# A two-layer hybrid decoder: products with V in pairs, branch weights split two tiles at once, two changes of order

## The chip, the cores and the metric

One core of a Trainium2 chip runs the whole kernel in one launch. The metric is the device time of that launch in microseconds (us); of several runs the median is taken.

## The reference, cut to what matters

Two layers, each on x of 512 tokens by 1024 channels, all in float32:

```
x = x + 1/2 SwiGLU(RMSNorm(x))
u = RMSNorm(x);  one projection u @ w_in feeds four branches and four merge gates
  A  sliding-window attention (8 heads, 2 K/V groups, window 128, sinks)
  B  gated short convolution
  C  three attentions (compressed, selected, windowed), 8 heads, 2 K/V groups, sigmoid gates
  D  retention, 4 heads, chunks of 128, group norm, swish gate
x = x + w_out( sum_b sigmoid(gate_b) * (y_b @ w_branch_b) )
x = x + 1/2 SwiGLU(RMSNorm(x))
```

Softmax rows P are multiplied with V: for each of the two K/V groups, `out[query, 64] += P[query, 128 keys] @ V[128 keys, 64]`, for four heads at once.

## The kernel before, in words

**Precision.** Weight matrices come in as float32 and are split in two by `split` (L206 to L215): ScalarE writes `whi` (L213), VectorE writes the rest, `wlo = raw - whi` (L214). Activations are split alike, so one product is three matmuls. `whi` and `wlo` have two buffers each in the pool `wp`; while `ph["two"]` holds, splits alternate between `wp` and the pool `fp`.

**Order.** The kernel is written through a framework that lists every engine's instructions by their place in the program and a planner's estimate of when each is ready, and then fixes that order. Every engine executes its own list strictly in order. `tc.issue_after(ins)` places an engine's later instructions behind `ins`.

**The mixer of a layer** (function `mixer`) goes in this program order: `swa_prep`, `swa` (branch A), `merge(1)` (branch B), `retention` (D), `merge(0)`, `nsa` (C), `merge(3)`, `merge(2)`, then w_out. What is later in the program fills gaps of what is earlier: the matmuls of a merge (L231 gate projections, L818 branch products) lie between the instructions of the attentions.

**Products with V** (`pv_acc`, L1070 to L1087). For block j of 128 keys, `turn(j)` makes for each group g four transposes of P on TensorE (L1076) into one PSUM tile `tp` (2 buffers), and one ScalarE copy to `PT` (L1078, 3 buffers). Then one matmul per group (L1086), V of 64 columns stationary, PT of 512 columns moving; group 0 writes partitions 0 to 63 of one PSUM tile `pv`, group 1 partitions 64 to 127. `turn(j + 1)` stands in the program ahead of the matmuls of j. Being float32, a matmul is recorded as two instructions. There are 1, 2, 2, 2 blocks for the four query blocks of `swa` and twice 1, 2, 3, 4 for those of `nsa`: 27 pairs in a layer.

**Merges** (`merge`). For each of 8 output tiles d: the gate (projected, or for `(b, c)` in `slots`, that is (2,0), (2,1), (1,1), (0,1), fetched by a GpSimd DMA into `th`, 2 buffers, L791), a split of a 512-wide piece of w_branch, 12 matmuls (L818), and on VectorE the gating and the sum into `merged` (L822, L823). In `merge(2)` the function `out_in` splits each finished `merged[d]` into a pair of halves of tiles `b` (L1253, L1254).

**w_out** (`out_unit`). Pool `mx`, which holds `merged`, is left and `fp` opened. Eight units d, each 24 matmuls over k = 0 to 7 (L1280); k needs the halves of `merged[k]`. The weights of four units are prepared ahead of the first.

**Retention's end.** `nsa` stands in `issue_after(mark["ret"].ins)`. `mark["ret"]` is the last transpose of retention's last chunk (L952), which needs `on` of VectorE (L948, L949), computed from `po` (L921, L923).

Of the kernel before, what the change touches and what calls it, by code (L numbers as in the profile page):

```python
# [12 lines left out]
AF = mybir.ActivationFunctionType  # L13
OP = mybir.AluOpType
AX = mybir.AxisListType

T = 512
D = 1024
NT = T // 128
KT = D // 128  # L20
# [51 lines left out]
def body(tc, ins, out):  # L72
# [620 lines left out]
    def mixer(l, spill, F):  # L693
# [89 lines left out]
        def merge(b, y, perm, done=None):  # L783
            yh, yl = y
            wb = ins["w_branch"][l, b]
            gen = weights_fm(w_in, O_MG + b * D, KT if (b, 1) not in slots else KT // 2)

            def gate(d):
                if (b, d // 4) in slots:
                    z = mp.tile([128, T], F32, name="th", tag="th", bufs=2)  # L790
                    pool.dma_start(z, gated[l][:, slots[b, d // 4] * 4 + d % 4])  # L791
                    return z
                ps = mm_t()
                dot(ps, next(gen), A, ks, True, True)
                z = mp.tile([128, T], F32, name="th", tag="th", bufs=2)
                dve.tensor_tensor(z, ps, R, op=OP.mult)
                act.activation(z, z, AF.Tanh, scale=0.5, bias=vcol("merge_gate_bias", (l * 4 + b) * KT + d))
                return z

            for c in range(2):  # L800
                raw = raw_t().rearrange("p (k n) -> p k n", k=4)
                cs = slice(c * 512, (c + 1) * 512)
                loaded = False
                for d in range(4 * c, 4 * c + 4):
                    z = gate(d)
                    if not loaded:
                        loaded = True
                        if perm:
                            for g in range(2):
                                sp.dma_start(raw[g * 64:(g + 1) * 64], wb[g * 256:(g + 1) * 256, cs].rearrange("(r d) n -> d r n", d=64))  # L810
                        else:
                            sp.dma_start(raw, wb[:, cs].rearrange("(k p) n -> p k n", p=128))
                    s = d - 4 * c
                    whi, wlo = split(raw[:, :, s * 128:(s + 1) * 128], (4, 128))
                    ps = mm_t()
                    for k in range(4):
                        for j, (x, v) in enumerate(((whi, yh), (whi, yl), (wlo, yh))):
                            pe.matmul(ps, x[:, k], v[:, k], start=k == 0 and j == 0, stop=k == 3 and j == 2)  # L818
                    if merge.first:
                        dve.scalar_tensor_tensor(merged[:, d], z, 1.0, ps, op0=OP.add, op1=OP.mult)  # L820
                    else:
                        dve.scalar_tensor_tensor(z, z, 1.0, ps, op0=OP.add, op1=OP.mult)  # L822
                        dve.tensor_tensor(merged[:, d], merged[:, d], z, op=OP.add)  # L823
                    if done:
                        done(d)
            merge.first = False
# [11 lines left out]
        def retention(ps_q, ps_k, ps_v, ps_g):  # L838
# [54 lines left out]
            for i in range(NT):  # L893
                rot, t = qk[i // 2][:, i % 2], sx[i // 2][:, i % 2]
                rf, tf = rot.rearrange("p h d -> p (h d)"), t.rearrange("p h d -> p (h d)")
                ps = tp_t()
                for c in range(4):
                    pe.transpose(ps[:, c * 128:(c + 1) * 128], rf[:, c * 128:(c + 1) * 128], ident)
                qkT = w2()
                act.activation(qkT, ps, AF.Copy)  # L900
                if i:
                    ps = tp_t()
                    for c in range(2):
                        pe.transpose(ps[:, c * 128:(c + 1) * 128], tf[:, c * 128:(c + 1) * 128], ident)
                    qxT = w2()
                    act.activation(qxT[:, :256], ps[:, :256], AF.Copy)

                at = w2()
                for par in range(2):
                    b0 = par * 64  # L910
                    ps = sc_t()
                    for c in range(2):
                        cs = slice(c * 128, (c + 1) * 128)
                        pe.matmul(ps[:, cs], qkT[b0:b0 + 64, 256 + c * 128:256 + (c + 1) * 128], qkT[b0:b0 + 64, cs], start=True, stop=True)
                    dve.tensor_tensor(at.rearrange("p (c q t) -> p c q t", c=2, q=2)[:, :, par], ps[:, :256].rearrange("p (c t) -> p c t", c=2),
                                      dmask.rearrange("p (c q) t -> p c q t", c=2)[:, :, par], op=OP.mult)
                po = pv_t()
                vi = v[i // 2][:, i % 2]
                for h in range(RH):
                    hs = slice(h * 128, (h + 1) * 128)  # L920
                    pe.matmul(po[:, hs], at[:, hs], vi[:, hs], start=True, stop=i == 0)  # L921
                    if i:
                        pe.matmul(po[:, hs], qxT[:, (h // 2) * 128:(h // 2 + 1) * 128], S[:, h], start=False, stop=True)  # L923
                if i < NT - 1:
                    ps = tp_t()
                    for h in range(RH):
                        b0 = (h % 2) * 64
                        pe.matmul(ps[b0:b0 + 64, (h // 2) * 128:(h // 2 + 1) * 128], t[:, 4 + h, :], vi[:, h * 128:(h + 1) * 128], start=True, stop=True)
                    for h in range(RH):
                        rows, c = slice((h % 2) * 64, (h % 2) * 64 + 64), h // 2  # L930
                        src = ps[rows, c * 128:(c + 1) * 128]
                        if i == 0:
                            dve.tensor_copy(S[rows, h], src)
                        else:
                            dve.scalar_tensor_tensor(S[rows, h], S[rows, h], C["decay"][rows, c:c + 1], src, op0=OP.mult, op1=OP.add)
                bs = small([128, RH * 6], name="bs", bufs=2).rearrange("p (h s) -> p h s", h=RH)
                mv = small([128, RH * 2], name="mv", bufs=2).rearrange("p (h s) -> p h s", h=RH)
                for h in range(RH):
                    dve.bn_stats(bs[:, h], po[:, h * 128:(h + 1) * 128])
                for h in range(RH):  # L940
                    dve.bn_aggr(mv[:, h], bs[:, h])
                vv = small([128, RH], name="vv", bufs=2)
                dve.tensor_scalar(vv, mv[:, :, 1], EPS, None, op0=OP.add)
                rs = rsqrt(vv, RH)
                on = w2()
                for h in range(RH):
                    hs = slice(h * 128, (h + 1) * 128)
                    dve.tensor_scalar(on[:, hs], po[:, hs], mv[:, h, 0:1], rs[:, h:h + 1], op0=OP.subtract, op1=OP.mult)  # L948
                dve.tensor_tensor(on, on, g[i // 2][:, i % 2], op=OP.mult)  # L949
                ps = tp_t()  # L950
                for h in range(RH):
                    mark["ret"] = pe.transpose(ps[:, h * 128:(h + 1) * 128], on[:, h * 128:(h + 1) * 128], ident)  # L952
                put_y(ps, (yh, yl), i)
            return (yh, yl), gates

# [114 lines left out]
        def pv_acc(pv, P, nblk, V, first, last):  # L1070
            def turn(j):
                pts = []
                for g in range(2):
# [1 line left out]
                    for r in range(4):  # L1075
                        pe.transpose(ps[:, r * 128:(r + 1) * 128], P[4 * g + r][:, j * 128:(j + 1) * 128], ident)  # L1076
                    pt = aq.tile([128, 512], F32, name="PT", tag="PT", bufs=3)
                    act.activation(pt, ps, AF.Copy)  # L1078
                    pts.append(pt)
                return pts  # L1080

            pts = turn(0)
            for j in range(nblk):
                nxt = turn(j + 1) if j + 1 < nblk else None
                for g in range(2):
                    pv_last[0] = pe.matmul(pv[g * 64:(g + 1) * 64], V(g, j), pts[g], start=first and j == 0, stop=last and j == nblk - 1)  # L1086
                pts = nxt  # L1087

        def swa_prep():
            return q_prep(O_AQ) + kv_prep(proj_tm(O_AK, 256), 1, [G["swa_k"]])  # L1090
# [177 lines left out]
        def out_unit(d):  # L1268
# [3 lines left out]
                return split(raws[d // 2][:, :, d % 2 * 128:(d % 2 + 1) * 128], (KT, 128), d < 4)  # L1272

            def run(w):
                whi, wlo = w
                ps = mm_t()
                for k in range(KT):
                    hi, lo = (t[k // 2][:, k % 2] for t in m)
                    for j, (x, v) in enumerate(((whi, hi), (whi, lo), (wlo, hi))):
                        pe.matmul(ps, x[:, k], v, start=k == 0 and j == 0, stop=k == KT - 1 and j == 2)  # L1280
                dve.scalar_tensor_tensor(XT[d], ps, 0.5, XT[d], op0=OP.mult, op1=OP.add)
                norm_in(d, vcol("ffn2_norm", l * KT + d), True)

            return prep, run

# [95 lines left out]
```

## Time and profile before

| what | value |
|---|---|
| median of 3 runs | 2796.18 us (2795.99 to 2796.74) |
| the profiled execution | 2791.7 us |
| its span, first to last instruction | 2789.9 us |
| granted TensorE clock, mean | 0.994 |
| DMA: moved, mean rate | 291.25 MB, 104 GB/s |

Stages of layer 1 in the span: attention A 555 to 608 us, retention 690 to 757, attention C 855 to 975, `merge(2)` 983 to 1009, w_out from 1014; layer 2 has the same some 1382 us later. A timeline row gives start, duration, engine, line, output<-inputs and a count where neighbours are merged; what stands in brackets is the idle time ahead of it and what ended that.

### The profile page before, as it was taken

The numbers are of one execution on the slowest core, as the hardware profiler recorded it, in microseconds if no ns is written. First come the engines' busy times: TensorE is split into PE (matmuls) and PEld (weight loads), VectorE is DVE, ScalarE is ACT, GpSimd is POOL, SyncE is SP. The second block draws the span as 40 slices with busy tenths as digits, with TensorE's granted clock in tenths as the row PEclk, the third lists the DMA queues.
The fourth block names the chain that finished last, engine by engine and source line by source line (L and its number), as shares of the span: only waits on it lengthen the run. The fifth ranks groups of instructions, "written<-read, shape, count | busy, mean of one in ns | idle before, by whom it ended". The sixth has DMA issues, their size and how long they took to land.

```text
span 2789.9 us, 42565 instructions
## 1 busy us (share of the span) xinstructions
PE 2751.5 (99%) x17303; PEld 2380.6 (85%) x17303; DVE 2087.7 (75%) x3490; ACT 1354.1 (49%) x2152; POOL 63.9 (2%) x70
## 2 busy tenths in 40 slices
PE   7999999999999989999999999999999999999999
PEld 7999999878776579999999998998787766799997
DVE  8887899664757569786897868896557575788874
ACT  7443565453246545443554435555432465554443
POOL 0000000000000010000000000000000000100000
PEclk9999999999999999999999999999999999999999
DMA  5233324414232052333323333334233221532322
GB/s 169 91 108 115 119 98 155 158 59 121 76 121 61 1 185 88 106 108 105 110 87 108 97 99 126 126 127 146 89 91 106 91 61 39 174 106 91 97 86 76
DMA packets 243336, 291.25 MB, mean 104 GB/s; under 512 B 8060, under 2 KB 211652, under 8 KB 241092
## 3 DMA queue, kind: packets, MB, share of 16 engines
q1 hardware_dynamic: 235604, 273.78, 30.3%
q0 software_dynamic: 3136, 12.59, 1.4%
q8 instruction: 135, 2.21, 0.3%
q10 hardware_dynamic: 4400, 2.17, 0.3%
q14 instruction: 61, 0.50, 0.1%
HBM read 269.64 MB, written 18.87 MB: 103 GB/s over the span
## 4 chain that ended last, share of the span: by engine, by line
PE 60%; DVE 2%; ACT 1%; issue 0%; DMA 0%; ACTq 0%; POOL 0%; DVEq 0%; POOLq 0%
PE sc L432 16%; PE mm L562 12%; PE tp L432 8%; PE mm L231 5%; PE pv L432 4%; PE mm L1280 3%; PE mm L818 3%; PE mm L777 3%; PE pv L1086 2%; PE tp L1076 1%; PE pv L777 1%; PE sc L1038 1%; PE sc L1039 1%; DVE wlo L214 0%; DVE Alo L343 0%
## 5 line engine op out<-in xcount | busy, mean ns | idle before, releaser
L213 ACT ACTIVATE whi<-raw 128x1024 fp32r<-128x1024 f32 (+2 forms) x354 | 337.2, 954 | 596.9 <-PE mm L562 122.4
L214 DVE TENSOR_TENSOR wlo<-raw,whi 128x1024 fp32r<-128x1024 f32 (+2 forms) x354 | 384.4, 1091 | 164.3 <-ACT whi L213 157.6
L562 PE MATMUL mm<-h,whi 128*128 128x512 f32 x1408 | 442.8, 395 | 0.0
L213 ACT ACTIVATE whi<-s 128x1024 fp32r<-128x1024 f32 x232 | 246.0, 1060 | 337.7 <-PE sc L432 77.5
L214 DVE TENSOR_TENSOR wlo<-s,whi 128x1024 fp32r<-128x1024 f32 x232 | 282.4, 1219 | 48.0 <-ACT whi L213 47.3
L562 PEld LDWEIGHTS mm<-h,whi 128*128 128x128 f32 x1408 | 259.9, 188 | 59.2 <-DVE h L549 0.2
L432 PE MATMUL sc<-E,whi 128*128 128x256 f32 x1856 | 297.0, 282 | 0.0
L562 PE MATMUL mm<-h,wlo 128*128 128x512 f32 x704 | 277.9, 395 | 0.0
L432 PEld LDWEIGHTS sc<-E,whi 128*128 128x128 f32 x1856 | 254.4, 191 | 0.0
L432 PE MATMUL sc<-E,wlo 128*128 128x256 f32 x928 | 186.5, 282 | 0.1
L566 DVE SCALAR_TENSOR_TENSOR XT<-mm,XT 128x512 f32<-128x512 f32 x128 | 88.0, 687 | 124.5 <-PE mm L562 124.5
L231 PE MATMUL mm<-Ahi,whi 128*128 128x512 f32 x416 | 167.8, 403 | 0.0
L432 PE MATMUL sc<-Ahi,whi 128*128 128x256 f32 x816 | 164.5, 283 | 3.3 <-ACT whi L213 3.3
L231 PE MATMUL mm<-Alo,whi 128*128 128x512 f32 x416 | 166.4, 400 | 0.0
L231 PE MATMUL mm<-Ahi,wlo 128*128 128x512 f32 x416 | 166.2, 400 | 0.0
L432 PE MATMUL sc<-Ahi,wlo 128*128 128x256 f32 x816 | 163.7, 282 | 0.5 <-DVE wlo L214 0.5
L432 PE MATMUL sc<-Alo,whi 128*128 128x256 f32 x816 | 163.9, 282 | 0.0
L562 PEld LDWEIGHTS mm<-h,wlo 128*128 128x128 f32 x704 | 132.0, 187 | 32.1
L213 ACT ACTIVATE whi<-rawd 128x1024 fp32r<-128x1024 f32 (+1 forms) x96 | 94.7, 988 | 131.4 <-PE sc L432 64.3
L432 PE MATMUL tp<-E,whi 128*128 128x256 f32 x928 | 147.8, 281 | 0.3 <-ACT sn L419 0.3
L432 PEld LDWEIGHTS sc<-E,wlo 128*128 128x128 f32 x928 | 143.8, 191 | 0.3 <-DVE wlo L214 0.3
L438 DVE TENSOR_TENSOR s<-raw 128x1024 f32<-128x1024 f32 x116 | 141.2, 1217 | 3.7 <-DMA raw<-in_ffn_w_up_dram 2.9
(318 smaller groups left out, 6113.3 us busy)
## 6 DMA issues: line engine op xcount, KB each, us to landing
raw<-in_w_in_dram SPq DMA_DIRECT2D x66, 1024.0 KB, 6.1
raw<-in_ffn_w_gate_dram SPq DMA_DIRECT2D x44, 1024.0 KB, 5.2
raw<-in_ffn_w_up_dram SPq DMA_DIRECT2D x44, 1024.0 KB, 7.7
rawd<-in_ffn_w_down_dram SPq DMA_DIRECT2D x32, 1024.0 KB, 5.3
rawd<-in_ffn_w_down_dram SPq DMA_DIRECT2D x16, 768.0 KB, 4.4
gs<-O SPq DMA_DIRECT2D x8, 1024.0 KB, 3.9
raw<-in_w_branch_dram SPq DMA_DIRECT2D x8, 1024.0 KB, 8.3
th<-gs POOLq DMA_DIRECT2D x32, 256.0 KB, 3.0
```

The lines of the kernel that those rows point to most:

```text
L213: act.activation(hi, src, AF.Copy)
L214: dve.tensor_tensor(lo, src, fv(hi), op=OP.subtract)
L231: pe.matmul(ps, x, y, start=first and j == 0, stop=last and j == len(passes) - 1)
L432: pe.matmul(ps[:, g * 256:(g + 1) * 256], x[:, g * 4 + c], factor(u, s, c), start=first and n == 0, stop=last and n >= 22, skip_group_chec ...
L438: dve.tensor_tensor(t, a, b, op=OP.add)
L562: pe.matmul(ps, x[:, k, j * 128:(j + 1) * 128], h[:, s, b], start=k == 0 and n == 0, stop=k == nf - 1 and n == 2)
L566: dve.scalar_tensor_tensor(XT[d], ps, 0.5, XT[d], op0=OP.mult, op1=OP.add)
L777: pe.matmul(ps[i][:, :n], a, w, start=kk == 0 and j == 0, stop=kk == KT - 1 and j == 2)
L818: pe.matmul(ps, x[:, k], v[:, k], start=k == 0 and j == 0, stop=k == 3 and j == 2)
L1038: pe.matmul(ps[:, :n], q, kT[0][:, g, s0:s0 + n], start=True, stop=False)
L1086: pv_last[0] = pe.matmul(pv[g * 64:(g + 1) * 64], V(g, j), pts[g], start=first and j == 0, stop=last and j == nblk - 1)
L1280: pe.matmul(ps, x[:, k], v, start=k == 0 and j == 0, stop=k == KT - 1 and j == 2)
```

## The change

Four edits. (1) In `pv_acc` the matmul of group 0 gets a dependency on the ScalarE copy of group 1, so that both matmuls of a block are ready together. (2) In `merge`, for tiles whose gates are fetched, a split takes 256 columns (two tiles) at a time. (3) In w_out, unit 0 stops after k = 5, unit 1 does k = 0 to 5, then unit 0 and unit 1 do k = 6 and 7. (4) `mark["ret"]` becomes the last chunk's last matmul of attention with V (L921) in place of the last transpose.

```diff
+SYNC = mybir.DependencyInfo(mybir.DependencyClass.Sync, mybir.DependencyReason.DATA)
...
-                    whi, wlo = split(raw[:, :, s * 128:(s + 1) * 128], (4, 128))
+                    if (b, c) in slots:
+                        if s % 2 == 0:
+                            two = split(raw[:, :, s * 128:(s + 2) * 128], (4, 256))
+                        whi, wlo = (t[:, :, s % 2 * 128:(s % 2 + 1) * 128] for t in two)
+                    else:
+                        whi, wlo = split(raw[:, :, s * 128:(s + 1) * 128], (4, 128))
...
-                    pe.matmul(po[:, hs], at[:, hs], vi[:, hs], start=True, stop=i == 0)
+                    mark["ret"] = pe.matmul(po[:, hs], at[:, hs], vi[:, hs], start=True, stop=i == 0)
...
-                    mark["ret"] = pe.transpose(ps[:, h * 128:(h + 1) * 128], on[:, h * 128:(h + 1) * 128], ident)
+                    pe.transpose(ps[:, h * 128:(h + 1) * 128], on[:, h * 128:(h + 1) * 128], ident)
...
-                    act.activation(pt, ps, AF.Copy)
+                    last_copy[0] = act.activation(pt, ps, AF.Copy)
                     pts.append(pt)
-                return pts
-
-            pts = turn(0)
+                return pts, last_copy[0]
+
+            last_copy = [None]
+            pts, copied = turn(0)
             for j in range(nblk):
-                nxt = turn(j + 1) if j + 1 < nblk else None
+                nxt = turn(j + 1) if j + 1 < nblk else (None, None)
                 for g in range(2):
                     pv_last[0] = pe.matmul(pv[g * 64:(g + 1) * 64], V(g, j), pts[g], start=first and j == 0, stop=last and j == nblk - 1)
-                pts = nxt
+                    if g == 0:
+                        tc.add_manual_dep(pv_last[0].ins, copied.ins.name, SYNC, reason="pair")
+                pts, copied = nxt
...
             def run(w):
-                whi, wlo = w
+                def mms(ps, w, k0, k1):
+                    whi, wlo = w
+                    for k in range(k0, k1):
+                        hi, lo = (t[k // 2][:, k % 2] for t in m)
+                        for j, (x, v) in enumerate(((whi, hi), (whi, lo), (wlo, hi))):
+                            pe.matmul(ps, x[:, k], v, start=k == 0 and j == 0, stop=k == KT - 1 and j == 2)
+
+                def done(d, ps):
+                    dve.scalar_tensor_tensor(XT[d], ps, 0.5, XT[d], op0=OP.mult, op1=OP.add)
+                    norm_in(d, vcol("ffn2_norm", l * KT + d), True)
+
                 ps = mm_t()
+                if d < 2:
+                    mms(ps, w, 0, KT - 2)
+                    if d == 0:
+                        raws["kept"] = ps, w
+                        return
+                    p0, w0 = raws.pop("kept")
+                    mms(p0, w0, KT - 2, KT)
+                    done(0, p0)
+                    mms(ps, w, KT - 2, KT)
+                else:
+                    mms(ps, w, 0, KT)
+                done(d, ps)
...
```

## Rows read from the trace of the kernel before

**Rows 1.** Busy time of each engine, share of the span and instructions, whole span.
```profile
PE 2751.5 (99%) x17303; PEld 2380.6 (85%) x17303; DVE 2087.7 (75%) x3490; ACT 1354.1 (49%) x2152; POOL 63.9 (2%) x70
```

**Rows 2.** Waits of PE, whole span: who for whom, us in total, times, longest.
```profile
PE tp L952 <- DVE w L949: 5.6, 2, 2.8
PE mm L1280 <- ACT whi L213: 5.2, 1, 5.2
PE mm L818 <- DVE wlo L214: 3.9, 2, 2.1
```

**Rows 3.** Timeline of PE, attention C of layer 1, last query block.
```profile
946.39 0.66 PE L1076 MATMUL tp<-ident,P 128*128 128x128 f32 x4
946.97 1.07 PE L1086 MATMUL pv<-PT,b 128*64 128x512 f32 x2
947.98 0.66 PE L1076 MATMUL tp<-ident,P 128*128 128x128 f32 x4
...
951.74 1.08 PE L1086 MATMUL pv<-PT,b 128*64 128x512 f32 x4
952.75 0.50 PE L1038 MATMUL sc<-b,b 128*128 128x512 f32 x1
...
971.56 1.93 PE L1086 MATMUL pv<-PT,b 128*64 128x512 f32 x6
```

**Rows 4.** Timeline of ACT in the same stretch.
```profile
947.14 0.60 ACT L1078 ACTIVATE PT<-tp 128x512 f32<-128x512 f32 x1 [0.99 <-PE tp L1076]
...
951.51 0.71 ACT L1054 ACTIVATE P<-P,nm 128x512 f32<-128x512 f32 x1
...
952.22 0.58 ACT L1078 ACTIVATE PT<-tp 128x512 f32<-128x512 f32 x1
```

**Rows 5.** Windows of attentions A and C, layer 1: all engines' busy time, clock, DMA.
```profile
555.00:608.00 53.00, 52.86 (x265) 35.24 (x264) 39.78 (x151) 37.20 (x111) 0.54 (x1) 1.00 0.13 41
855.00:975.00 120.00, 119.80 (x548) 72.11 (x548) 81.28 (x287) 72.44 (x179) 0.00 (x0) 1.00 0.13 36
```

**Rows 6.** Window behind attention C: PE of L231, then of L818.
```profile
973.50:983.30 9.80, 5.61 (x24) 4.51 (x24) 1.00 0.48 111
...
973.50:983.30 9.80, 4.51 (x19) 3.59 (x20) 1.00 0.48 111
```

**Rows 7.** Timeline of PE at retention's end, layer 1.
```profile
751.78 0.39 PE L818 MATMUL mm<-E,wlo 128*128 128x512 f32 x1
754.94 0.93 PE L952 MATMUL tp<-ident,w 128*128 128x128 f32 x4 [2.78 <-DVE w L949]
```

**Rows 8.** Windows behind it, PE of L231: busy (count), PEld, granted clock, DMA.
```profile
755.50:758.50 3.00, 2.97 (x7) 2.42 (x8) 0.50 0.29 92
759.00:762.00 3.00, 3.00 (x15) 2.47 (x14) 1.00 0.00 0
```

**Rows 9.** Groups of VectorE by form: the low half, 1024 and 512 wide.
```profile
L214 DVE TENSOR_TENSOR wlo<-raw,whi 128x1024 fp32r<-128x1024 f32 x266 | 323.5, 1223 | 129.9 <-ACT whi L213 123.8 <-PE mm L231 3.1
...
L214 DVE TENSOR_TENSOR wlo<-raw,whi 128x512 fp32r<-128x512 f32 x80 | 55.0, 687 | 24.9 <-ACT whi L213 24.4
```

**Rows 10.** Timeline of DVE in `merge(2)`, layer 1.
```profile
998.32 0.69 DVE L822 SCALAR_TENSOR_TENSOR th<-th,mm 128x512 f32<-128x512 f32 x1 [3.97 <-DMA th<-gs]
998.92 0.68 DVE L214 TENSOR_TENSOR wlo<-raw,whi 128x512 fp32r<-128x512 f32 x1
```

**Rows 11.** Timeline of PE there and at w_out's start.
```profile
999.66 0.50 PE L818 MATMUL mm<-E,wlo 128*128 128x512 f32 x1 [1.82 <-DVE wlo L214]
...
1014.50 1.16 PE L1280 MATMUL mm<-b,whi 128*128 128x512 f32 x2 [5.16 <-ACT whi L213]
```

**Rows 12.** Timeline of ACT at w_out's start, layer 1, then the DMA queue SP.
```profile
1012.87 0.63 ACT L1253 ACTIVATE b<-merged 128x512 fp32r<-128x512 f32 x1 [2.61 <-DVE merged L823]
1013.41 1.99 ACT L213 ACTIVATE whi<-raw 128x1024 fp32r<-128x1024 f32 x2
...
990.30 1.04 SPq L220 DMA_DIRECT2D raw<-in_w_out_dram  x2
```

More of the change, by code (lines that the diff above doesn't have):

```diff
@@ L1274, in run @@
             def run(w):
-                whi, wlo = w
-                ps = mm_t()
[L1277 to L1282, printed above, removed]
+                def mms(ps, w, k0, k1):
[7 more added lines that the diff above has]
+                    norm_in(d, vcol("ffn2_norm", l * KT + d), True)
+                ps = mm_t()
+                if d < 2:
[10 more added lines that the diff above has]
+                done(d, ps)
             return prep, run
```

## The prediction

> **What bounds the kernel now.** I read four views in this order. First the busy times of the whole span: TensorE is busy for 2751.5 of 2789.9 us, VectorE for three quarters, ScalarE for half [rows 1]. So time can only come from less work on TensorE or from its few waits. Second the waits of TensorE: of those that the edits touch there are three, 5.6 us in two places for retention's last transposes, 5.2 us in one place at w_out, 3.9 us in two places inside a merge [rows 2]. Third the timeline of TensorE in attention C, for the price of a product with V: the reader is to see four transposes, then one product (two records), in turn, with no gap. A product alone starts at 946.97 and the next instruction at 947.98, so it takes 1.01 us; where two products of different groups were both ready (951.74, x4) the next starts at 952.75, again 1.01 us for both [rows 3]. Fourth the same stretch by engine: in attentions A and C TensorE is busy for 52.9 of 53 and 119.8 of 120 us, VectorE and ScalarE for about two thirds [rows 5]. TensorE is the bound there, filled by matmuls of the merges.
>
> All sums are made against the profiled execution, 2791.7 us with a span of 2789.9; the median of the three runs, 2796.18, lies 4.5 us above it. I carry the difference over to the median unchanged.
>
> **Edit 1, pairs.** Rows 3 show one row of x4 and one of x6; each layer has 4 of x4 and 5 of x6. The x6 row holds a pair and a single product, 1.93 us long; a product lasts 1.07 where its successor starts after 1.01, so it takes 1.87 [rows 3]. Of a layer's 54 products 4 x 2 + 5 x 3 = 23 lie in these rows, 31 are single. TensorE spends 31 x 1.01 + 4 x 1.01 + 5 x 1.87 = 44.7 us. With all 27 pairs side by side it is 27 x 1.01 = 27.3. The upper end is 17.4 us a layer.
>
> A rule speaks for less. By the Trainium skill, "TensorE: Matmul & The Clock Gate", Part 3, "Measured speedup vs the span model", three column tiles ran 2.38 times as fast as one after another, about 0.79 each. By it, an estimate from that page, two products would take 2.02 / 1.59 = 1.27 us and not 1.01. The row of two products in 1.01 us decides against it.
>
> The price is waiting. The first product of a pair now waits for the second copy, 0.60 us [rows 4]. In a chain of several blocks a new cycle appears, because three PT buffers let the copy of (j+1, group 1) start only after pair j: pair 1.07, hand-over 0.09 (transposes end 947.05, copy starts 947.14), copy 0.60, hand-over back at most 0.24 (copy ends 947.74, transposes start 947.98, where TensorE was busy anyway), four transposes with their switch 0.58 (946.39 to 946.97): about 2.6 us a block [rows 3, 4]. The work on TensorE in it is 1.01 + 0.58 + 0.44 (the second four without a switch, an estimate from 0.66 - 0.22 of overhang): 2.0. Before, a block took 2 x 1.59 = 3.2 (946.39 to 947.98, twice). So 0.55 us a block is uncovered. Chains of 2, 3, 4 blocks have 1, 2, 3 such cycles; a layer has 5, 2, 2 of them, 15 cycles, 8 us. The first pair of each of 12 chains may wait 0.60 more, 7 us. If nothing covers these 15 us, edit 1 gives 17.4 - 15 = 2.4 us a layer: the lower end.
>
> The cover is matmuls of the merges. In A they last far beyond its end, so I take 3 of A's 4 us (28 of the 108 records are A's). In C 9.8 us of them are left over behind it: 24 of L231 and 19 of L818 [rows 6]. But C's chain is not shortened as much as its TensorE work: softmax of the next group waits for the transposes that free P, and these come only about 0.7 to 1.3 us earlier in a chain of four, about 4 us over C (an estimate from the cycles above). C's 13.3 us come in full only if the planner draws all 9.8 us into the gaps. Between 4 and 13.3 I take 8. Edit 1: 11 us a layer, **22** in all, ends 5 and 35.
>
> **Edit 4, retention's end.** TensorE ends the merge's products, then idles 2.78 us until VectorE delivers the last `on`; branch C's first matmul (L231) stands behind those transposes [rows 7]. In the wake the granted clock is 0.50, the 1.2 GHz level: 7 matmuls in 3 us against 15 at 1.00, so about 1.6 us are lost [rows 8]. With the mark on L921, ten us earlier, L231 may fill the wait; its weights are split by then. The upper end is 2.78 + 1.6 = 4.4 a layer. The lower end is 0: the transposes go first in the program, and if the planner thinks them ready as soon as the merge ends, TensorE waits for them as before. Nothing excludes a small loss, 0.5, by splits of C ahead of `on` on VectorE. I take 3 a layer, **6** in all; what is late next is nothing, since D's result is used only in `merge(3)`.
>
> **Edit 2, splits.** 32 splits of 512 become 16 of 1024: VectorE 32 x 0.687 = 22.0 against 16 x 1.223 = 19.6, 2.4 us less, ScalarE alike [rows 9]; hidden everywhere but in `merge(2)`, where VectorE is not the bound of anything. There the odd tile's `wlo` stands on VectorE behind a gating step that waits 3.97 us for a `th` DMA [rows 10], and TensorE waits 1.82 us for it [rows 11]; both layers together 3.9 [rows 2]. The stalled tile is the second of its pair, so its `wlo` will have been made one tile earlier: this wait goes, and with it about 1.6 us of half clock as in rows 8. The next one moves to the end: w_out's weights queue on ScalarE behind the split of `merged[7]`, which waits for VectorE and so for the same `th` chain [rows 12]. TensorE only arrives earlier at that. What can shorten the chain is the raw tile: the two w_out loads that run against the `th` DMAs start at 990.30 when a branch tile is released [rows 12], now some 5 us earlier, for `wlo` of tiles 2 and 3 is made with one split. Bounds a layer: a gain of 3.5 (the whole stall), a loss of 1.5 (the contention hits `th` of earlier tiles). I take 2 a layer, **4** in all.
>
> **Edit 3, w_out.** No instruction is added. In layer 1 the first matmul waits 5.16 us for the weights of unit 0, which are split last, at 1013.41 [rows 11, 12]; units 0 and 1 both need weights, so stopping unit 0 after k = 5 helps only if unit 1's weights are the early ones and the planner puts it first. Layer 2 has no such wait: rows 2 count it once. There unit 1's k = 0 to 5 may now wait for weights while k = 6 and 7 of unit 0 (6 matmuls, 1.4 us at 15 in 3 us [rows 8]) could have run. Between +1.4 and -2 a layer I take **0**.
>
> **Sum.** 22 + 6 + 4 + 0 = 32. Profiled execution 2760; median 2796.2 - 32 = **2764 us**.
>
> **Rivals.**
>
> *Full cover.* Every gap takes a merge matmul, and retention's wait closes: 35 + 9 + 4 = 48, 2748 us. For it: TensorE is gapless today [rows 5] by the same planner. Against: the merge work runs out just behind C [rows 6].
>
> *The wait eats the pair.* The gaps stay open as in the lower end: 5 from edit 1, 6 from the rest, about 2785 us. For it: order is fixed by estimates that do not know that two products run in 1.01, so TensorE arrives at each wait early. Against: single products stood in the trace only where the copy was late, and there the planner did fill.
>
> *Slower: TensorE's queue blocked by ScalarE.* The second copy can stand behind exponentials: at 952.22 a copy followed one of 0.71 and its 0.19 read-out [rows 4]. TensorE then stops with all that is queued behind: transposes, scores, merge matmuls. With copy and one exponential, 1.5 us, uncovered at each of 54 pairs, the loss is 81 against 35 + 10 gained: 2832 us; it decides from 45 / 54 = 0.83 us a pair. Against: most copies start 0.09 us after their transposes.
>
> *Pairs do not run side by side at full speed.* With 1.27 us a pair edit 1's upper end falls to 44.7 - 34.3 = 10.4 a layer, and the time to about 2775. Against it stand 18 stretches of the kind of rows 3, all of 1.01.
>
> **How the numbers follow.** Forecast case (2754 to 2774) 0.53; full cover (down to 2745) 0.13; wait eats the pair (2774 to 2790) and slower pairs 0.19 and 0.03; within 0.2% (5.6 us, about what a measurement of this kernel can tell from no change) 0.06; slower 0.06. Hence faster 0.88. The range 2748 to 2784 leaves out about half of the full cover and a third of the weak case.
>
> **What would show it.** Edit 1: 54 rows of L1086 with x4, none single, and the busy time of L1086 down by a third; the gaps ahead of L1086 and L1076 for PT give its price, above 0.3 us a pair on average my 22 is too high. Edit 4: L952 no longer in the list of waits, clock 1.00 behind it. Edit 2: no wait of L818 for `wlo`. Edit 3: the wait ahead of the first L1280 in layer 1 still there, about 5 us or longer, and perhaps a new one in layer 2. The prediction is wrong if attention C does not end at least 4 us earlier relative to its start, or if new waits for PT exceed 15 us a layer.

## The result, and the profile after

The changed kernel takes **2745.6 us** (median of 4 runs, 2744.4 to 2747.4) where the kernel before takes 2796.1: ratio 0.982, 95% interval 0.981 to 0.984. Forecast were 2764 us, range 2748 to 2784. The direction was right, the gain is 50 us instead of 32, and the time lies 2.4 us below the range. A second measurement of the same kernel, beside the experiments, gave 2750.6 (ratio 0.984, 0.983 to 0.986), inside the range; both say that 2764 was too high. The profiled execution of after is 2744.4 us long, its span 2742.3.

TensorE's busy time, below (engine: busy us, share of the span, instructions), fell by 41.8 us against [rows 1] with the same 17303 instructions. 35.5 of them are products with V that now run side by side: L1093 is busy for 58.3 us where L1086 was busy for 93.8.

```profile
PE 2709.7 (99%) x17303; PEld 2369.4 (86%) x17303; DVE 2089.4 (76%) x3474; ACT 1347.0 (49%) x2136; POOL 63.5 (2%) x70
```

TensorE's waits of after (who for whom: us in total, times, longest), the rows that answer to [rows 2]. Retention's transposes wait 0.4 instead of 5.6, the wait for `wlo` inside a merge is gone, the one at w_out has grown from 5.2 to 7.1, and a new one of 1.2, in layer 2, waits for a half of `merged`:

```profile
PE mm L1290 <- ACT whi L214: 7.1, 1, 7.1
...
PE mm L1290 <- ACT b L1263: 1.2, 1, 1.2
...
PE tp L958 <- DVE w L955: 0.4, 1, 0.4
```

Timeline of TensorE in attention C of layer 1, last query block, the place of [rows 3] (start, us, engine, line, operation, out<-in, form, count). Every product is a pair (x4; in the whole trace 54 times, none single), the next pair starts 2.41 us later, and in the gap of each cycle shown lies exactly one matmul of the next merge (L232):

```profile
930.04 1.08 PE L1093 MATMUL pv<-PT,b 128*64 128x512 f32 x4
931.05 0.66 PE L1082 MATMUL tp<-ident,P 128*128 128x128 f32 x4
931.46 0.48 PE L232 MATMUL mm<-Ahi,wlo 128*128 128x512 f32 x1
931.86 0.66 PE L1082 MATMUL tp<-ident,P 128*128 128x128 f32 x4
932.45 1.08 PE L1093 MATMUL pv<-PT,b 128*64 128x512 f32 x4
933.46 0.66 PE L1082 MATMUL tp<-ident,P 128*128 128x128 f32 x4
933.87 0.48 PE L232 MATMUL mm<-Ahi,whi 128*128 128x512 f32 x1
```

ScalarE beside it, as [rows 4]: twice a run of two copies waits, 1.32 and 1.22 us, for the pair that frees a buffer of `PT`. This is the cycle that the prediction described; it is there, but covered.

```profile
931.21 1.19 ACT L1084 ACTIVATE PT<-tp 128x512 f32<-128x512 f32 x2 [1.32 <-PE pv L1093]
933.62 1.19 ACT L1084 ACTIVATE PT<-tp 128x512 f32<-128x512 f32 x2 [1.22 <-PE pv L1093]
```

The whole of C in layer 1, from its first score to its last product, by engine (window, its length, then busy us and instructions of PE, PEld, DVE, ACT, POOL; granted clock, DMA share, GB/s), of before and of after. C is 8.06 us shorter, without a gap, and holds 24 matmuls more:

```profile
848.79:972.90 124.11, 123.91 (x578) 76.12 (x577) 86.12 (x313) 76.38 (x193) 0.00 (x0) 1.00 0.12 35
```

```profile
840.28:956.33 116.05, 115.94 (x602) 77.87 (x602) 89.24 (x316) 75.87 (x194) 0.54 (x1) 1.00 0.20 56
```

These 24 were left over behind C in [rows 6]; there now stand 7 of L232 and 13 of L824 (rows below, with one of each that began in C) instead of 24 and 19:

```profile
955.85:961.07 5.22, 1.72 (x7) 1.05 (x6) 1.00 0.24 77
...
955.85:961.07 5.22, 2.72 (x13) 2.44 (x13) 1.00 0.24 77
```

At retention's end, the place of [rows 7], C's first projection (L232) follows the previous merge at once, the transposes lie among its matmuls, and behind them the granted clock stays at 1.00, the 2.4 GHz level, with 15 matmuls in 3 us, where [rows 8] had 7 at 0.50:

```profile
747.80 0.39 PE L824 MATMUL mm<-E,wlo 128*128 128x512 f32 x1
748.03 0.39 PE L232 MATMUL mm<-Ahi,whi 128*128 128x512 f32 x1
...
751.07 0.63 PE L958 MATMUL tp<-ident,w 128*128 128x128 f32 x4
```

```profile
752.00:755.00 3.00, 3.00 (x15) 2.46 (x14) 1.00 0.02 5
```

At w_out's start in layer 1 the wait has not gone but moved with the rest: the split of the late weights starts at 989.48, TensorE has been idle since 983.47, and its first stretch of w_out runs at half clock (7 matmuls in 3 us, later 14), the places of [rows 11, 12]:

```profile
983.08 0.39 PE L824 MATMUL mm<-E,wlo 128*128 128x512 f32 x1
990.57 1.22 PE L1290 MATMUL mm<-b,whi 128*128 128x512 f32 x2 [7.10 <-ACT whi L214]
```

```profile
988.94 0.63 ACT L1263 ACTIVATE b<-merged 128x512 fp32r<-128x512 f32 x1 [2.23 <-DVE merged L829]
989.48 1.99 ACT L214 ACTIVATE whi<-raw 128x1024 fp32r<-128x1024 f32 x2
```

```profile
991.00:994.00 3.00, 2.96 (x7) 1.85 (x7) 0.50 0.73 242
998.00:1001.00 3.00, 3.00 (x14) 2.44 (x13) 1.00 0.99 337
```

**Where the time went.** Each stretch runs between the starts of two TensorE instructions in the profiled executions; the entries are its change against before, layer 1 / layer 2, in us.

| stretch | after | edit 1 alone | edit 2 alone | edit 4 alone |
|---|---|---|---|---|
| A, first score to last product | -2.8 / -2.9 | -2.8 / -2.9 | 0 / 0 | 0 / 0 |
| to retention's last product | -0.9 / -0.9 | -1.4 / -1.4 | +0.4 / +0.4 | 0 / 0 |
| to C's first score | -5.0 / -4.6 | -0.2 / -1.2 | -2.0 / 0 | -4.6 / -4.6 |
| C, first score to last product | -8.1 / -8.0 | -8.1 / -7.5 | 0 / +0.3 | 0 / 0 |
| to the last branch product | -9.3 / -9.6 | -5.5 / -5.9 | -3.6 / -3.9 | +0.4 / -0.7 |
| to w_out's first product | +1.9 / 0 | +0.1 / 0 | +2.3 / 0 | 0 / 0 |
| w_out, to its last product | +0.1 / +1.8 | +1.3 / 0 | +0.7 / +2.3 | +0.1 / +1.2 |

Entries of one or two us in w_out also differ between profiles of one kernel (layer 2 of after: +1.8 here, +3.8 in its second profile); I read those that are larger or alike in both layers.

### The profile page after: what moved, and what is told of

The parts are those of the page before. It is cut to its first block, busy times and chain, and to the rows that moved or that the text cites. A ratio compares the mean times of both kernels' runs of the same rounds, so it can differ in the third digit from the quotient of the medians.

```text
span 2742.3 us, 42536 instructions
## 1 busy us (share of the span) xinstructions
PE 2709.7 (99%) x17303; PEld 2369.4 (86%) x17303; DVE 2089.4 (76%) x3474; ACT 1347.0 (49%) x2136; POOL 63.5 (2%) x70
## 4 chain that ended last, share of the span: by engine, by line
PE 51%; issue 9%; DVE 2%; ACT 1%; DMA 1%; POOL 0%; ACTq 0%; POOLq 0%; DVEq 0%
PE sc L433 16%; PE mm L563 12%; PE tp L433 8%; PE pv L433 4%; PE mm L1290 3%; PE mm L232 3%; PE mm L824 1%; PE pv L1093 1%; PE tp L1082 1%; PE mm L778 1%; PE sc L1044 0%; DMA th<-gs 0%; PE sc L1045 0%; DVE wlo L215 0%; DVE Alo L344 0%
## 5 line engine op out<-in xcount | busy, mean ns | idle before, releaser
L232 PE MATMUL mm<-Ahi,whi 128*128 128x512 f32 x416 | 168.0, 404 | 0.0
L232 PE MATMUL mm<-Alo,whi 128*128 128x512 f32 x416 | 167.4, 402 | 0.0
L232 PE MATMUL mm<-Ahi,wlo 128*128 128x512 f32 x416 | 166.4, 400 | 0.0
```

The lines of the kernel that those rows point to most:

```text
L232: pe.matmul(ps, x, y, start=first and j == 0, stop=last and j == len(passes) - 1)
```

## The experiments

Theory: the step that failed is the cover of edit 1's waits; merge matmuls fill all of them, so the pair is worth its whole TensorE time. Rival: edit 1 gave its 22 and the other edits gave 28 instead of 10.

### Each edit alone

The kernel before plus one edit. The runs are numbered in another order than the edits.

```
e1   tc.add_manual_dep(pv_last[0].ins, copied.ins.name, SYNC, ...)   (edit 1, the pairs)
e2   mark["ret"] = pe.matmul(po[:, hs], at[:, hs], ...)              (edit 4, order at retention's end)
e3   two = split(raw[:, :, s * 128:(s + 2) * 128], (4, 256))         (edit 2, splits of two tiles)
e4   mms(ps, w, 0, KT - 2) ... mms(p0, w0, KT - 2, KT)               (edit 3, w_out's late finish)
```

> The kernel before with edit 1 alone: both groups' products with V side by side, the first one waiting for both copies. Theory (full cover: merge matmuls fill every gap in which the pair waits, so the pair saves all its TensorE time): 54 pairs x 0.59 us less some queue time, about 17 us a layer, 33 to 36 us below before, so 2760 to 2763. Rival (the pair gives the 22 us that were forecast, because part of the wait stays open, and the other edits together gave about 28): 2772 to 2777. In the trace the theory wants TensorE's wait for the copies of P below 3 us in all and the products with V at one pair per block in about 1.0 us; the rival wants 8 us or more of waits for the copies.

> The kernel before with edit 4 alone: the compressed branch is held back only by retention's last product, not by its last transposes. Theory: the stall of 2.8 us and the two stretches at half clock at retention's end go in both layers, 4.4 us a layer, so about 9 us below before: 2787. Rival (the 3 a layer that were taken): about 6 us below, 2790. If edit 1 was what removed the half clock there, the gain is under 4 us.

> The kernel before with edit 2 alone: the branch weights of the attached merges split two tiles at once. Theory: the wait of 1.95 us a layer for the low half ahead of the branch products goes and the products behind attention run without stretches at half clock, 1.5 to 3.5 us a layer: 3 to 7 us below before, 2789 to 2793. Rival (the stall goes only because edit 1 moved those products into attention's gaps, where nobody waits for the split): no difference, 2795 to 2797.

> The kernel before with edit 3 alone: the first two tiles of w_out stop after six of eight steps and are finished behind each other. Theory: in layer 1 tile 0's weights come late and the first product of w_out waits as before, in layer 2 tile 1's come late, so the order helps there at most by 1 us or hurts: between 2795 and 2799. Rival (the two tiles cover the last halves of the merged vectors): 2 us a layer less, about 2792.

| kernel | median us | against 2795.8 before | ratio, 95% interval |
|---|---|---|---|
| edit 1 | 2760.2 | -35.7 | 0.987 (0.986 to 0.989) |
| edit 4 | 2787.3 | -8.5 | 0.997 (0.996 to 0.998) |
| edit 2 | 2793.5 | -2.3 | 0.999 (0.998 to 1.000) |
| edit 3 | 2796.8 | +1.0 | 1.000 (0.999 to 1.001) |

Edit 1 gives what the theory asked; the rival falls. Its C in layer 1 is that of after (same count, same length):

```profile
846.26:962.30 116.04, 115.93 (x602) 77.84 (x602) 89.21 (x316) 75.85 (x194) 0.54 (x1) 1.00 0.21 57
```

Edit 4 gives close to its upper end, 8.5 of 8.8. Edit 2 can't be told from nothing by its time; its trace shows why. The stall inside the merge goes (-3.6 and -3.9 in the table), and part comes back at w_out. In layer 1 TensorE arrives there earlier and waits 2.3 longer for the same split: 7.4 in the row below where [rows 2] had 5.2. In layer 2 w_out's own stretch is 2.3 longer, and TensorE waits 1.6 there for the last half of `merged`. That wait comes with edit 2: every kernel with it has the wait in layer 2 (1.2 to 1.9) except e8 below, and no kernel without it does, edit 3 alone included.

```profile
PE mm L1285 <- ACT whi L213: 7.4, 1, 7.4
...
PE mm L1285 <- ACT b L1258: 1.6, 1, 1.6
```

Edit 3 alone does nothing that can be measured. The four add to 45.4.

### The price of the pair without cover

In both kernels the merge whose matmuls fill C's gaps (the fill) is issued only behind C's last product; e6 also has edit 1.

```diff
-        merge(3, yd, False)
+        with tc.issue_after(pv_last[0].ins):
+            merge(3, yd, False)
```

> The kernel before, with the third merge (retention's branch) issued only behind the last product with V, so that none of its matmuls can stand in the gaps of attention C. Theory (these matmuls are what fills the gaps): the kernel becomes slower by what TensorE then idles in C, 5 to 20 us a layer: 2806 to 2836. Rival (the gaps are short anyway in the order of before): under 5 us in all, below 2801.

> The same with edit 1 added: pairs, and no merge matmuls in C's gaps. Theory (edit 1's gain in C depends on the fill: without it each block waits about 0.55 us for the second copy): C gains little, A keeps its 3 us a layer, so 5 to 18 us below the run with single products and without the fill, and TensorE waits for the copies of P 8 us or more a layer in C. Rival (the pair's wait is covered by its own next transposes, the fill is not needed): 26 to 36 us below it, with waits for the copies below 4 us a layer.

Without fill the kernel takes 2900.8 us with single products and 2874.9 with pairs, 25.9 apart; before takes 2796.2 beside them. The loss of 104.6 is larger than I expected: the displaced merge makes the stretch behind C 54 us longer in each layer, while C itself grows by 1.0 and 4.3. So C carries this merge almost free. My theory on the pair falls here: C loses 9.6 and 11.2 us a layer by pairing even without fill (first score to last product, 125.14 to 115.56 in layer 1), and TensorE's waits for the copies of P come to 9.6 us in all, against 7.9 in e5, not 8 a layer. The rival is nearly met and not quite: it asked for 26 us and waits below 4 a layer, where 25.9 and 4.8 came. In C of layer 1, e5 and then e6, TensorE's work falls by 15.0 us, the stretch by 9.6; its idle time grows from 13.2 to 18.7 us:

```profile
847.28:972.42 125.14, 111.92 (x416) 56.80 (x417) 70.68 (x291) 66.09 (x179) 0.00 (x0) 0.86 0.00 1
```

```profile
842.75:958.31 115.56, 96.90 (x417) 54.54 (x417) 71.86 (x291) 65.83 (x179) 0.00 (x0) 0.85 0.00 1
```

What grows most is not the wait for the copies (`PT`, 7.9 and then 9.6 us) but the one for the softmax rows that VectorE finishes (`P`), 4.0 and then 13.6 us in all, e5 and then e6:

```profile
PE pv L1086 <- ACT PT L1078: 5.2, 10, 0.7
...
PE tp L1076 <- DVE P L1067: 4.0, 4, 1.6
...
PE tp L1076 <- ACT PT L1078: 2.7, 6, 0.5
```

```profile
PE tp L1077 <- DVE P L1068: 13.6, 14, 3.0
...
PE tp L1077 <- ACT PT L1079: 7.8, 18, 0.7
...
PE pv L1088 <- ACT PT L1079: 1.8, 4, 0.7
```

Where the granted clock is 1.00, the cycle is the same with and without fill. In e5 a product and its transposes take 1.59 us, a block twice that, 3.18; in e6 pairs follow each other after 2.40, as they do in after (2.41):

```profile
944.70 1.07 PE L1086 MATMUL pv<-PT,b 128*64 128x512 f32 x2
945.70 0.66 PE L1076 MATMUL tp<-ident,P 128*128 128x128 f32 x4
946.29 1.07 PE L1086 MATMUL pv<-PT,b 128*64 128x512 f32 x2
```

```profile
953.60 1.08 PE L1088 MATMUL pv<-PT,b 128*64 128x512 f32 x4
954.61 0.66 PE L1077 MATMUL tp<-ident,P 128*128 128x128 f32 x4
955.41 0.66 PE L1077 MATMUL tp<-ident,P 128*128 128x128 f32 x4 [0.15 <-ACT PT L1079]
956.00 1.08 PE L1088 MATMUL pv<-PT,b 128*64 128x512 f32 x4
```

So C's part needs no fill: 9.6 and 11.2 us a layer without it, 8.1 and 7.5 with it. With fill, another 5.5 and 5.9 come from merge matmuls that leave the stretch behind C (table above). A gives its 2.8 and 2.9 in e6 too, but A's own fill was not taken out, so whether that part needs cover is not shown.

### Parts taken out of the changed kernel

The changed kernel without edit 3 (e7), once more as it is (e9), without edit 2 (e10), without edit 1 (e12); each edit is undone to the lines of before.

> The changed kernel without edit 3: w_out's tiles each finished before the next begins. Theory (edit 3 puts tile 1's first six steps ahead of tile 0's last two, and in layer 2 tile 1's weights are the late ones): 0 to 4 us faster than the changed kernel, 2742 to 2746. Rival (the late finish hides the last halves of the merged vectors): 2 to 4 us slower, 2747 to 2750.

> The changed kernel itself once more, beside the three that follow, so that they are compared on one chip. Both theories: 2743 to 2748.

> The changed kernel without edit 2. Alone, edits 1, 4, 2 and 3 gave -35.7, -8.5, -2.3 and +1.0, together 45.4, where the changed kernel gave 50.5. Theory (edit 2 is worth more where edit 1 has drawn the merge into attention C and edit 3 takes back what it costs at w_out): 5 to 9 us slower than the changed kernel, 2750 to 2755. Rival (edit 1 moves the branch products into the gaps anyway, so nobody waits for the split; the 5 us are scatter of the medians): 0 to 4 us slower, 2745 to 2749.

> The changed kernel without edit 1: edits 2, 3 and 4 on single products. Theory (edit 1 is worth its full TensorE time, 35 us, wherever it stands): 34 to 40 us slower than the changed kernel, 2780 to 2786. Rival (edits 2 to 4 together give the rest that was not forecast, edit 1 no more than 30): below 2776.

e9 to e12 were measured side by side, so they are compared with e9. The changed kernel again: 2750.6, above what both theories wanted. In the profiled executions, 2.6 of 6.7 us more had gathered before attention A, in the first feed-forward, which no edit touches; the kernels measured here begin A anywhere from 557.4 to 560.5. What sets this is open. Without edit 1: 2783.6, 33.0 more, one below the theory's 34, far from the rival's bound. Without edit 2: 2751.5, 0.9 more, as the rival has it, though for another reason: the wait for `wlo` is back (row below) and the stretch behind C is 2.9 us a layer longer, while the stretches from there to w_out's last product take 1.5 less in layer 1 and 2.7 less in layer 2 than in e9. Without edit 3: 2749.3, between the two measurements of the changed kernel, so no effect that can be told.

```profile
PE mm L819 <- DVE wlo L215: 4.7, 4, 2.2
```

### The wait at w_out

The wait of 7.1 us remained. Weights of w_out's units alternate between two pools, and one of them is only free when the last half of `merged` has been taken. Unit 0 falls into that pool in layer 1, unit 1 in layer 2. Here units 0 and 1 get the free pool (e8), and the same without edit 3 (e11):

```diff
         def prep():
+            ph["flip"] = d % 4 < 2
```

> The changed kernel, with the weights of w_out's tiles 0 and 1 put into the buffers that are free early, and those of tiles 2 and 3 into the ones that the merged vectors hold until their last half is taken. Theory: the wait of 7.1 us ahead of w_out's first product in layer 1 goes and so does its half-clock stretch; in layer 2 a wait of 1.2 us: 6 to 9 us below the changed kernel, about 2738. Rival (the splits are ScalarE's and VectorE's work in any buffer, and the halves of the merged vectors then end later by as much): within 2 us of it.

> The kernel with the weights of w_out's tiles 0 and 1 in the early buffers (2737.7), without edit 3. Theory (with both tiles' weights there in time, edit 3's order covers the last half of the merged vectors, whose split comes 1 to 2 us late in each layer): 2 to 5 us slower than with edit 3, 2740 to 2743. Rival (edit 3 does nothing in either buffer order): within 2 us, 2736 to 2740.

e8 takes **2737.7 us** (ratio to before 0.979, 0.978 to 0.980): 7.9 below the changed kernel's first measurement, 12.9 below its second, below both intervals, and 11.6 below e7, which was measured beside it. It beats both kernels. e11, beside e9, takes 2741.7 (0.981, 0.980 to 0.982), 8.9 below e9. In e8 w_out's first product follows the last branch product:

```profile
982.90 0.39 PE L824 MATMUL mm<-E,wlo 128*128 128x512 f32 x1
983.13 0.63 PE L1291 MATMUL mm<-b,whi 128*128 128x512 f32 x2
```

and its first stretch runs at full clock, 14 matmuls in 3 us:

```profile
984.00:987.00 3.00, 3.00 (x14) 2.40 (x14) 1.00 0.30 87
```

In e11 the next wait shows, for the last half of `merged`; edit 3's order covers it in e8:

```profile
992.62 0.50 PE L1291 MATMUL mm<-b,whi 128*128 128x512 f32 x1 [1.73 <-ACT b L1263]
```

So edit 3 covers a wait only once the weights are there: e11 waits 1.7 and 1.2 us for that half, e8 in neither layer. What it is worth, 4.0 by the medians and 3.1 in the stretches from the last branch product to w_out's last product (2.0 and 1.1), is no more than the two measurements of the changed kernel differ (5.0).

## Why the prediction was wrong, by its own steps

**Edit 1, the step that failed: "Between 4 and 13.3 I take 8".** Attention C as a whole was said to become about 4 us shorter, because P is freed earlier, and the rest to come only if the left-over matmuls are drawn in. Alone, edit 1 made C 8.1 and 7.5 us shorter and drew in another 5.5 and 5.9: 13.6 and 13.4, the upper end. A's side came in full too (2.8 and 1.4 behind it, where I took 3 of 4). A layer gave 16.5 and 18.9 against the upper end of 17.4. Instead of 22 it was 35.7 (33.0 when taken out).

The step took the earlier release of P for all that shortens C. That release was sized well. A chain is the row of products that belongs to one softmax; from the transposes with which its second group begins to its last transposes, the eight chains of a layer took 36.1 us in all before and 32.4 after, 3.7 less where about 4 was said. The two chains of four give 1.3 and 1.9 of it (0.7 to 1.3 was said); the first of them in layer 1, before and then after:

```profile
942.78 0.93 PE L1076 MATMUL tp<-ident,P 128*128 128x128 f32 x7
...
951.15 0.66 PE L1076 MATMUL tp<-ident,P 128*128 128x128 f32 x4
```

```profile
927.21 0.82 PE L1082 MATMUL tp<-ident,P 128*128 128x128 f32 x6
...
934.27 0.66 PE L1082 MATMUL tp<-ident,P 128*128 128x128 f32 x4
```

What the step put at nothing are the stretches between the chains, from a chain's last transposes to the next one's second group: seven in a layer, 76.1 us in all before and 70.7 after, 5.3 and 5.4 less in the two layers. At C's end 1.1 is lost. Without fill these stretches give 9.3 of the 9.6 and 9.1 of the 11.2. What gets shorter in them no run isolates; that stays open.

The uncovered part of a cycle was put at 0.55; in the cycles shown it is 0.40 (931.46 to 931.86), the place of one matmul, and one stands in each. The cycle itself, 2.6 forecast and 2.41 measured, and the buffer that closes it were right (the hand-over back was put at up to 0.24 and is 0.06: the first copy ends at 931.80), as was the pair in 1.01 us: pair starts at 930.04, next instruction at 931.05. By the Trainium skill, "TensorE: Matmul & The Clock Gate", Part 3, "Measured speedup vs the span model", three column tiles together ran 2.38 times as fast as one after another. No run here has three; the estimate of 1.27 us that carries this over to two does not agree with the trace, where two 64-column float32 products take 1.01 us, as one does.

Two readings of the rows were loose, without weight for the result. A fifth row of x4 in each layer (860.00, 1.83 long) was counted as two single products, 2.02 us where 1.76 pass to the next start. And of the 18 stretches called "all of 1.01" eight take 1.01; the ten of x6 hold three products in 1.86.

**Edit 4.** I took 3 of 4.4 a layer; 4.6 and 4.6 came, 8.5 us by the medians. The planner did not put the transposes first, so the lower bound's reason did not hold. The half clock went with the wait.

**Edit 2.** The stall goes in full, as stated (3.6 to 3.9 against the bound of 3.5), but "the next one moves to the end" had a price that I left out of the value taken: 2.3 us of layer 1's 3.6 return at w_out, and in layer 2 a wait of 1.6 for the last half of `merged` out of 3.9. Instead of 4 it is 2.3 alone and 0.9 when taken out, neither clear of nothing. The w_out loads did start earlier (963.91 instead of 990.30), which did not help: the late weights wait for a free buffer behind the last half of `merged`, not for their raw tile, as e8 shows by giving them another buffer.

**Edit 3.** 0 forecast, none measured; the wait ahead of w_out's first product in layer 1 is there, 7.1. The new wait in layer 2 that was held possible here is another one, for a half of `merged`, and comes with edit 2.

**The rivals.** "Full cover", 2748 us at a chance of 0.13, is nearly what happened, 2.4 us from the first measurement; of its terms edit 1's 35 and edit 4's 9 came, edit 2's 4 did not. That TensorE was gapless under the same planner spoke for it and deserved more; what I held against it, that merge work runs out behind C, was no reason: 43 matmuls were left over there, 24 were needed. ScalarE blocked nothing: waits for the copies were to exceed 15 us a layer in that case, and the list of after's waits has no row for them. Of the rest, about 5 us between the sum of the single edits, 45.4, and the first measurement, 50.5, stays open; the second, 44.7, agrees with the sum.

## What to carry to other kernels

In this kernel TensorE had no gaps and an independent stretch of work was left over right behind, and a saving on TensorE was worth its whole duration. So count the instructions that are left over against the time freed, and take a discount only for what they can't fill. When one step of a chain gets shorter, ask what that does to the stretches between the chains as well: here they gave more than the chains themselves. And a stall that is removed ahead of a later wait was only worth what that wait did not return: follow the late operand to the buffer that it needs (at w_out this was worth more than edits 2 and 3 together).

## What the runs showed of the hardware

Two products with V of 64 stationary columns, writing different halves of the partitions, take 1.01 us together (930.04 to 931.05), as long as one alone [rows 3]. Behind such a product, four transposes take 0.41 us when a matmul with 128 stationary columns follows (931.05 to 931.46) and 0.58 when a product with 64 follows (946.39 to 946.97 in [rows 3]): the product costs about 0.17 us to enter, now once for two products instead of once for each. What takes this time no run isolates. And with the fill taken out of C of layer 1, TensorE was idle for 13.2 of 125.1 us there and its mean granted clock was 0.86, where before it was idle for 0.2 of 124.1 and the clock was 1.00.
